# The first two pairs of the input projection k tile by k tile, the norms' squares and their weights moved, and y_b first in the attention

## The chip, the cores and the metric

One NeuronCore of one Trainium2 chip runs the whole kernel. The metric is the device time of one execution in microseconds (us). The five engines of the core work side by side, each through its own queue in order: TensorE (PE, with its weight loads shown apart as PEld), VectorE (DVE), ScalarE (ACT), GpSimd (POOL) and SyncE (SP), which here only issues DMAs.

## The reference, cut to what matters

One layer of a streaming encoder over 1024 tokens of width 1024, in float32:

```
h = rms_norm(x, norm_mix_pre)
q, k, v, u, gates = split(h @ w_in)            # 512 + 512 + 512 + 512 + 2048 columns
y_a = chunk_band_attention(q, k, v) @ w_attn_out   # 8 heads of 64, relative bias
y_b = multiscale_pool(u) @ w_pool_out
g_a, g_b = sigmoid(gates + b_gate)
x = x + rms_norm((g_a * y_a + g_b * y_b) @ w_o)
x = x + rms_norm(conv_gated_ffn(rms_norm(x)))
```

## The kernel before, in words

Every product is made of float32 numbers split in two (a high part rounded to the matmul's type, and the rest): `split` casts on ACT (line 78) and subtracts on DVE or POOL (line 79), and `mm3` (line 85) issues three matmuls of 128 x 128 by 512 columns for each k tile: high weight by high token, high by low, low by high. A block of 128 output columns over 512 tokens and all 8 k tiles is 24 matmuls.

The input projection runs over 16 pairs of output blocks (`IN_PAIRS`); each pair's weights are one load of 1 MB. Pairs 2 to 15 use a seven-product scheme of 2 x 2 blocks (class `Pair`, methods p1 to p7) on normalised, pre-added tokens (B11, T1, T2 and so on), which DVE and ACT make. Pairs 0 and 1 don't wait for the norms: they multiply the raw tokens (only scaled by the norm weights, `split_raw`, line 382), and the result is scaled per token afterwards (`evict_first`, line 437). The index i is the half of the k tiles (0 or 1, four tiles each), the index t or j the half of the tokens.

The order at the start (lines 358 to 371) is written out by hand: SP loads the tokens of (i, j) = (0, 0) in two pieces, all small columns (`cv`, 110 KB, with the norm weights in them), the weights of pairs 0 and 1 in pieces, the other token quarters, and then the eight row tiles `xn` for the norms. Lines 559 to 584 then do the products half by half: all of pair 0 for the first token half and i = 0 (bank X), pair 1 (bank Y), then i = 1, then the second token half (banks Z and Y). ACT takes the squares of all rows (`squares`, line 411), DVE makes the reciprocal roots (`scales`), `spread` lays them along the partitions through four PE transposes (line 424) and a DVE copy (line 426), and `normalise` (line 431) scales the raw tokens in place for the later pairs. The framework's list scheduler sets the order on each engine from the order of the program, from priorities (`tc.high_priority`) and from its own estimate of readiness.

PSUM has eight banks; a pool of tiles takes them in the order in which its tags are first named. In the projection that is X (banks 0, 1), Y (2, 3), Z (4, 5), m (6, 7). The attention's pools follow in the order psT (transposes, 2 banks), psf (y_b and the values, 2 banks), psS (scores, 2 x 2 banks), so that scores lie over Z and m. SBUF is used again in the same way: the attention's pool `atn` starts where the projection's operands T1, B11, B21, T2, ... lay, 16 KB for each high and low pair.

At the projection's end the last pair (products p1, p2, p6, p3, p7, p4 in this order) makes q and k of heads 6 and 7; `store_split` (lines 455 to 463) writes high and low parts with two DMAs each, for the last pair from POOL's queue. The attention goes through 32 steps (8 heads, 4 groups J of 256 queries) with the stages scores (lines 733, 742, softmax on DVE, ACT and POOL in 749 to 754), transposes (line 775) one step later, and values (line 800) two steps later. The pool branch's product y_b, cut in 32 units of 6 matmuls (tile ybp), is laid between them by a list `NU` written by hand, which says how many units each step takes. `load_head` loads q and k of a head (lines 705 to 709), `load_yb` a block of w_pool_out and the gates.

Of the kernel before, what the change touches and what calls it, by code (L numbers as in the profile page):

```python
# [10 lines left out]
F32 = mybir.dt.float32  # L11
F32R = mybir.dt.float32r
# [5 lines left out]
P = 128  # L18
# [3 lines left out]
DH = 64  # L22
# [11 lines left out]
C_GAIN = 212  # L34
NCOL = 220
# [12 lines left out]
def trunk(ctx, tc, xn, xt, w_in, cols, bias, w_ao, w_pg, w_po, w_o, gains, w_up, w_dn, out):  # L48
# [239 lines left out]
    def rstd_of(r, ssq, tmp, n, off=eps):  # L288
# [5 lines left out]
        A.activation(s, ssq, AF.Sqrt, scale=1.0 / D, bias=off)  # L294
# [7 lines left out]
        V.tensor_tensor(r, r, a, ALU.mult)  # L302

# [15 lines left out]
    with ExitStack() as ph:  # L319
# [33 lines left out]
        wr = [raw_tile(f"win{pi}") for pi in range(2)]  # L353
        wv = [w.rearrange("p (f q k c) -> p f q (k c)", f=2, q=2, k=4) for w in wr]
        wd = [w_in[pi].rearrange("p (f q n) -> p f q n", f=2, q=2) for pi in range(2)]
        q = {(i, j): raw_tile(f"xq{i}{j}").rearrange("p (k n) -> p k n", k=4)
             for j in range(2) for i in range(2)}
        nc.sync.dma_start(q[0, 0][:, 0:2], xt[0, 0][:, 0:2])
        nc.sync.dma_start(cv, cols)
        nc.sync.dma_start(wv[0][:, 0, 0], wd[0][:, 0, 0])  # L360
        nc.sync.dma_start(q[0, 0][:, 2:4], xt[0, 0][:, 2:4])
        nc.sync.dma_start(wv[0][:, 1, 0], wd[0][:, 1, 0])
        nc.sync.dma_start(wv[1][:, :, 0], wd[1][:, :, 0])
        nc.sync.dma_start(q[1, 0], xt[1, 0])
        for pi in range(2):
            nc.sync.dma_start(wv[pi][:, :, 1], wd[pi][:, :, 1])
# [9 lines left out]
        def gain(i, k):  # L376
            return cv[:, C_GAIN + 4 * i + k:C_GAIN + 4 * i + k + 1]

        def split_raw(i, j):
            hi, lo = XR[i, j]  # L380
            for k in range(4):
                A.activation(hi[:, k], q[i, j][:, k], AF.Identity, scale=gain(i, k))
                V.scalar_tensor_tensor(lo[:, k], q[i, j][:, k], gain(i, k), hi[:, k].bitcast(F32),
                                       ALU.mult, ALU.subtract)
# [3 lines left out]
        def split_in(pi, i):  # L388
            w = wr[pi].rearrange("p (f q k c) -> p f q k c", f=2, q=2, k=4)
            place = (lambda: tmp.tile([P, 2, 4, P], F32R, tag="o", name="w0s", bufs=4)) if pi == 0 else None  # L390
            for f in range(2):
                ws[pi, f, i] = split_w(w[:, f, i], f"i{pi}_{i}{f}", None, place)

        def half_in(pi, t, i, tag, fs=range(2)):


            for f in fs:
                if i == 0:
                    acc[pi, t, f] = psp.tile([P, 512], F32, tag=tag, name=f"i{pi}_{f}{t}")
                wh, wl = ws[pi, f, i]  # L400
                th, tl = XR[i, t]
                mm3(acc[pi, t, f], [wh[:, k] for k in range(4)], [wl[:, k] for k in range(4)],
                    [th[:, k] for k in range(4)], [tl[:, k] for k in range(4)], i == 0, i == 1)
# [5 lines left out]
        def squares(j):  # L409
# [3 lines left out]
        def scales(j):  # L413
            s = slice(4 * j, 4 * j + 4)
            rstd_of(rst[:, s], ssq[:, s], tmp, 4)

        def spread(j):

            s = slice(4 * j, 4 * j + 4)
            bc = tmp.tile([P, 4, P], F32, tag="S", name=f"bc{j}", bufs=4)  # L420
            V.tensor_copy(bc, rst[:, s].unsqueeze(2).to_broadcast([P, 4, P]))
# [4 lines left out]
            V.tensor_copy(Rb[j], ps)  # L426
# [38 lines left out]
        def evict_in(fb):  # L465
            def evict(f, t, ps, add):
# [10 lines left out]
                elif b < 16:  # L477
                    A.copy(d, ps)
# [821 lines left out]
```

## Time and profile before

| | |
|---|---|
| median of 3 runs | 1275.87 us (1274.69 to 1276.26) |
| the profiled execution | 1275.48 us |
| its span in the trace | 1273.7 us |
| TensorE (PE) busy | 1245.4 us, 98% |
| VectorE (DVE) busy | 907.6 us, 71% |
| ScalarE (ACT) busy | 667.3 us, 52% |
| GpSimd (POOL) busy | 313.9 us, 25% |

The profile is of one execution; its times start at the span's start. The share of an engine is an average over stages with different limits, so the views by stage and the list of waits say more than this table. The ends of matmuls are modelled: the distance between two starts is the sure quantity, not the length of one.

### The profile page before, as it was taken

Reading aid. Unit: us, or ns where it says so; the run is one execution under the profiler, and the core shown is the slowest. Engines: PE = TensorE matmul, PEld = TensorE weight load, DVE = VectorE, ACT = ScalarE, POOL = GpSimd, SP = SyncE. Lnnn points to the kernel's source line nnn. Section 1 sums busy time; section 2 is a strip of 40 time slices with the busy share of each in tenths; the row PEclk is TensorE's granted clock in tenths of the full one; section 3 lists DMA queues with packets and bytes.
Section 4 is the critical chain, followed back from the end, with each engine's and each line's share of the span. In section 5 each row is a group of like instructions: output and inputs, shape, how many; then the busy total and the mean of one; then the engine's idle time right before and its main releaser. Section 6 shows DMA issues by size and latency. Waiting matters only on the chain.

```text
span 1273.7 us, 16331 instructions
## 1 busy us (share of the span) xinstructions
PE 1245.4 (98%) x5780; PEld 1030.3 (81%) x5780; DVE 907.6 (71%) x1455; ACT 667.3 (52%) x1163; POOL 313.9 (25%) x270
## 2 busy tenths in 40 slices
PE   7999999999899999999999999999999999999997
PEld 6768887878788898888887888888888887888886
DVE  5894335875477777854799666666666676899958
ACT  7653245554477774433456555455455554445553
POOL 0005222322256556000034333333333310000000
PEclk9999999999999999999999999999999999999999
DMA  9345015344878965612142221221221259202103
GB/s 361 122 161 186 34 58 201 118 145 151 258 224 253 273 190 216 238 67 84 66 165 100 99 95 55 99 99 51 99 96 45 99 176 370 107 17 100 34 1 132
DMA packets 55857, 173.40 MB, mean 136 GB/s; under 512 B 5472, under 2 KB 6112, under 8 KB 50784
## 3 DMA queue, kind: packets, MB, share of 16 engines
q1 hardware_dynamic: 49424, 157.68, 35.8%
q10 hardware_dynamic: 4608, 8.39, 1.7%
q0 software_dynamic: 1744, 6.29, 1.3%
q8 instruction: 45, 0.74, 0.2%
q14 instruction: 36, 0.29, 0.1%
HBM read 125.16 MB, written 47.19 MB: 135 GB/s over the span
## 4 chain that ended last, share of the span: by engine, by line
PE 87%; DVE 6%; issue 3%; ACT 2%; DMA 1%; POOL 0%; DVEq 0%; ACTq 0%; SPq 0%; POOLq 0%
PE X_u L85 16%; PE X_i L85 9%; PE X L85 9%; PE Y_u L85 8%; PE wops L986 7%; PE Y L85 6%; PE Y_i L85 5%; PE Z_u L85 4%; PE y L85 4%; PE ybp L85 3%; PE i L85 3%; PE u L85 3%; PE f L800 2%; PE Z_i L85 2%; PE tp L775 2%
## 5 line engine op out<-in xcount | busy, mean ns | idle before, releaser
L1062 DVE SCALAR_TENSOR_TENSOR hc<-hu,cv,hc 128x1022 f32<-128x1022 f32 (+1 forms) x88 | 116.0, 1322 | 35.3 <-ACT hc L1057 35.2
L78 ACT CAST wh_u<-s_u 128x512 fp32r<-128x512 f32 x80 | 49.4, 618 | 78.7 <-PE Y_u L85 38.1
L79 DVE TENSOR_TENSOR wl_u<-s_u,wh_u 128x512 fp32r<-128x512 f32 x80 | 57.0, 714 | 39.8 <-ACT wh_u L78 39.7
L195 POOL TENSOR_TENSOR s_u<-wup 128x512 f32<-128x512 f32 x20 | 36.4, 1822 | 172.8 <-DMA wup<-in_w_up 127.1
L78 ACT CAST wh_u<-wup 128x512 fp32r<-128x512 f32 x72 | 44.6, 622 | 61.2 <-PE Y_u L85 29.0
L79 DVE TENSOR_TENSOR wl_i<-s_i,wh_i 128x512 fp32r<-128x512 f32 x56 | 41.4, 742 | 43.7 <-ACT wh_i L78 43.6
L78 ACT CAST wh_i<-s_i 128x512 fp32r<-128x512 f32 x56 | 34.7, 622 | 68.3 <-PE X_i L85 28.0
L199 POOL TENSOR_TENSOR s_u<-s_u,wup 128x512 f32<-128x512 f32 x20 | 28.1, 1407 | 137.6 <-DVE wl_u L79 137.5
L1057 ACT ACTIVATE hc<-hu,cv 128x1024 f32<-128x1024 f32 x44 | 54.6, 1243 | 10.9 <-DVE hu L1047 8.5
L195 POOL TENSOR_TENSOR s_i<-win 128x512 f32<-128x512 f32 x12 | 18.0, 1497 | 146.5 <-DVE wl_i L79 101.6
L79 DVE TENSOR_TENSOR wl_u<-wup,wh_u 128x512 fp32r<-128x512 f32 x72 | 50.4, 700 | 4.8 <-PE tp L311 2.0
L79 DVE TENSOR_TENSOR ptl<-tp,pth 128x512 fp32r<-128x512 f32 (+3 forms) x80 | 43.7, 555 | 13.7 <-ACT pth L78 12.5
L201 POOL TENSOR_TENSOR s_u<-wup 128x512 f32<-128x512 f32 x20 | 45.5, 2274 | 30.5 <-DVE wl_u L79 30.5
L754 POOL TENSOR_SCALAR pe<-pe,st 128x640 f32<-128x640 f32 (+2 forms) x64 | 43.0, 675 | 33.2 <-DVE st L753 28.3
L751 ACT ACTIVATE pe<-sm,st 128x640 f32<-128x640 f32 (+2 forms) x64 | 44.6, 698 | 6.3 <-DVE st L749 5.4
L78 ACT CAST wh_i<-win 128x512 fp32r<-128x512 f32 x42 | 25.7, 621 | 41.2 <-PE X_i L85 21.8
L1067 ACT ACTIVATE hc<-hc 128x1024 f32<-128x1024 f32 x22 | 23.4, 1064 | 40.6 <-DVE hc L1062 40.6
L749 DVE CUSTOM_DVE_ANT_0 sm<-pst,bt 128x640 f32<-128x640 f32 (+2 forms) x64 | 40.6, 651 | 4.2 <-PE pst L733 1.5
L85 PE MATMUL ybp<-mx,wh_yb 128*128 128x512 f32 x128 | 43.3, 418 | 0.0
L78 ACT CAST pth<-tp 128x512 fp32r<-128x512 f32 (+3 forms) x80 | 37.0, 472 | 9.4 <-PE tp L775 7.0
L775 PE MATMUL tp<-ident,pe 128*128 128x128 f32 x240 | 37.2, 278 | 0.4
L800 PE MATMUL f<-ptl,vv 128*128 128x256 f32 x144 | 36.8, 287 | 0.0
(521 smaller groups left out, 4193.9 us busy)
## 6 DMA issues: line engine op xcount, KB each, us to landing
wup<-in_w_up SPq DMA_DIRECT2D x22, 1024.0 KB, 4.9
win<-in_w_in SPq DMA_DIRECT2D x14, 1024.0 KB, 5.3
g_d<-hc SPq DMA_DIRECT2D x20, 512.0 KB, 2.6
sig_d<-d ACTq DMA_DIRECT2D x32, 256.0 KB, 2.0
a<-g_d SPq DMA_DIRECT2D x8, 1024.0 KB, 6.3
b<-in_w_dn SPq DMA_DIRECT2D x8, 1024.0 KB, 8.1
x<-in_xn SPq DMA_DIRECT2D x8, 512.0 KB, 12.8
v_d<-vt SPq DMA_DIRECT2D x8, 512.0 KB, 3.0
```

What stands on the lines that cost most here:

```text
L78: A.copy(hi, src)
L79: (eng or V).tensor_tensor(lo, src, hi.bitcast(F32), ALU.subtract)
L85: nc.tensor.matmul(ps, a[i], b[i], start=start and i == 0 and p == 0, stop=stop and i == n - 1 and p == 2, skip_group_check=True,)
L195: self.eng.tensor_tensor(self.s1, self.w21, self.w22, ALU.add)
L201: self.eng.tensor_tensor(self.s3, self.w11, self.w21, ALU.subtract)
L751: A.activation(pe[:, :n], sm[:, :n], AF.Exp, scale=-1.0, bias=st[:, 0:1], accum_out=st[:, 1:2])
L754: G.tensor_scalar(pe[:, :n], pe[:, :n], st[:, 2:3], 1.0, ALU.mult, ALU.mult)
L775: nc.tensor.transpose(tp[:, c * P:(c + 1) * P], pe[:, b * P:(b + 1) * P], ident)
L800: nc.tensor.matmul(fo, vv[:, kb, e].rearrange("p a d -> p (a d)"), t[:, s], start=s == slots[0] and x == 0, stop=s == slots[-1] and x == 1)
L986: nc.tensor.matmul(ps[:, 512 * c:512 * c + 512], a[k // 4][:, k % 4, sl], wo[k][b][:, 512 * c:512 * c + 512], start=k == 0 and x == 0, sto ...
L1057: A.activation(c, hu, AF.Identity, scale=cv[:, C_CW + 88 + b:C_CW + 89 + b], bias=cv[:, C_CB + b:C_CB + b + 1])
L1062: V.scalar_tensor_tensor(c[:, n:], hu[:, :S - n], cv[:, w:w + 1], c[:, n:], ALU.mult, ALU.add)
```

## The change

The diff below is cut to its core. In words:

- The weights of pairs 0 and 1 come in a layout of their own (`w_first`: for each k tile the 4 blocks of 128 columns side by side), and are loaded with the tokens k tile by k tile: pieces of 256 KB for the first two k tiles, 512 KB for the others. The norm weights become a load of 4 KB of their own (`gain_pre`) on ACT's queue; `cv` without them goes to the end of the opening loads, behind four of the row tiles, the second token half and the other four row tiles.
- For the first token half all four blocks (banks X, X, Y, Y) are done k tile by k tile, with the three products of a tile in the order high-high for the 4 blocks, high-low for the 4, low-high for the 4. ACT's instructions keep the order of the program here (`manual_schedule`): splits of the 8 k tiles, squares and root of the first four row tiles, raw split of the second half's i = 0, copy of the spread scales (now on ACT), raw split of i = 1, squares and root of the other four. The sigmoids of the first evictions come behind that second root.
- For the second half, blocks 0 and 1 (bank Z) go first, k tile by k tile, then blocks 2 and 3 one after the other (bank Y).
- `normalise` of the second half moves behind p2 of pair 2, and `evict_first(0, 1)` ahead of it.
- The tags of PSUM are named in the order m, Y, X, Z, and the attention's pools in the order psS, psT, psf: scores lie over m and Y, transposes over X, y_b and values over Z.
- `store_split` writes both parts with one DMA of SP, for the last pair too. One ACT instruction with Exp behind an eviction of pair 12 loads the exponential's table there.
- In the attention `load_yb(0)`, `load_head(0)`, the split of the first y_b weights and the scores of step 0 get high priority. The y_b weights move from pool `wrp` into `atn`, whose first tile they become. `NU` becomes 2, 2, 0, 1, 0, 1, 1, 2, then as before; the units of steps 0 and 1 are held behind the last score matmul of the step named in the diff.

```diff
 ...
+        for tag in "mYXZ":
+            psp.tile([P, 512], F32, tag=tag, name=f"bank{tag}")
+        gn = const.tile([P, 8], F32, name="gn")
+        A.dma_start(gn, gain_pre)
+        for c in (slice(0, 1), slice(1, 2), slice(2, 4)):
+            nc.sync.dma_start(q[0, 0][:, c], xt[0, 0][:, c])
+            nc.sync.dma_start(wr[0][:, c], w_first[0][:, c])
+        for c in (slice(0, 2), slice(2, 4)):
+            nc.sync.dma_start(q[1, 0][:, c], xt[1, 0][:, c])
+            nc.sync.dma_start(wr[1][:, c], w_first[1][:, c])
+        for n in range(4):
+            nc.sync.dma_start(xts[n], xn[n])
         for i in range(2):
             nc.sync.dma_start(q[i, 1], xt[i, 1])
-        for n in range(8):
+        for n in range(4, 8):
             nc.sync.dma_start(xts[n], xn[n])
+        nc.sync.dma_start(cv, cols)
 ...
+        def products(bs, t, i, k):
+            wh, wl = ws[i, k]
+            th, tl = XR[i, t]
+            for p, (w, x) in enumerate(((wh, th), (wh, tl), (wl, th))):
+                for b in bs:
+                    nc.tensor.matmul(acc[b, t], w[:, b], x[:, k], start=i == k == p == 0,
+                                     stop=i == 1 and k == 3 and p == 2, skip_group_check=True)
 ...
             Rb[j] = out_tile(f"R{j}")
-            V.tensor_copy(Rb[j], ps)
+            A.copy(Rb[j], ps)
 ...
+                kk = [(i, k) for i in range(2) for k in range(4)]
+                for b, tag in enumerate("XXYY"):
+                    bank(b, 0, tag)
+                with tc.manual_schedule(engines={nc.scalar.engine}):
+                    for i, k in kk:
+                        split_raw(i, 0, k)
+                        split_first(i, k)
+                        if (i, k) != kk[-1]:
+                            products(range(4), 0, i, k)
+                    load_win(2)
+                    load_win(3)
+                    scales(0)
+                    for k in range(4):
+                        split_raw(0, 1, k)
+                    spread(0)
+                    products(range(4), 0, 1, 3)
+                    for k in range(4):
+                        split_raw(1, 1, k)
+                    root = scales(1)
+                for b in range(2):
+                    bank(b, 1, "Z")
+                with tc.issue_after(root.ins):
+                    evict_first(1, 0)
+                    evict_first(0, 0)
                 for i in range(2):
                     normalise(i, 0)
+                for n, (i, k) in enumerate(kk):
+                    products(range(2), 1, i, k)
+                    if n == 4:
+                        spread(1)
+                for b in (2, 3):
+                    bank(b, 1, "Y")
+                for b in (2, 3):
+                    for i, k in kk:
+                        products((b,), 1, i, k)
 ...
                 pair.p1()
                 operand("B21", q[1, 0])
+                evict_first(0, 1)
                 pair.p2()
+                for i in range(2):
+                    normalise(i, 1)
                 nxt.p1()
 ...
-            eng.dma_start(hd, hi.bitcast(F32))
-            eng.dma_start(ld, lo.bitcast(F32))
+            nc.sync.dma_start(dst.rearrange("a p n -> p a n"), d.bitcast(F32))
 ...
+                if (f, t, fb) == (1, 1, IN_PAIRS[-4]):
+                    A.activation(warm, d[:, :1], AF.Exp, scale=0.0)
 ...
         atn = pool(ph, "attn", 2)
+        psS = pool(ph, "psS", 2, space=PSUM)
         psT = pool(ph, "psT", 2, space=PSUM)
         psf = pool(ph, "psf", 1, space=PSUM)
-        psS = pool(ph, "psS", 2, space=PSUM)
 ...
-            wr = load_block(w_po, m, "yb")
-            sg = sgs[m] if m in sgs else atn.tile([P, S], F32, tag="sg", name=f"sgb{m}")
+            wr = atn.tile([P, 4, P], F32, tag="wy", name=f"wr_yb{m}")
+            nc.sync.dma_start(wr, w_po[m])
+            sg = atn.tile([P, S], F32, tag="sg", name=f"sgb{m}")
 ...
-        load_head(0)
-        load_yb(0)
+        with tc.high_priority():
+            load_yb(0)
+            load_head(0)
+            first_yb = split_w(ybs[0][1], "yb0", V)
+            pend = {0: scores(0, 0)}
 ...
-        NU = [0, 1, 1, 2] * 7 + [0, 1, 1, 1, 1, 0]
+        NU = [2, 2, 0, 1, 0, 1, 1, 2] + [0, 1, 1, 2] * 5 + [0, 1, 1, 1, 1, 1]
 ...
+            if i == 1:
+                with tc.issue_after(last["pst"].ins):
+                    for _ in range(NU[i]):
+                        next(units)
             if 1 <= i <= len(steps):
                 transposed(steps[i - 1][1], pend.pop(i - 1))
-            for _ in range(NU[i]):
-                next(units, None)
+            if i == 0:
+                with tc.issue_after(last["pst"].ins):
+                    for _ in range(NU[i]):
+                        next(units)
+            elif i > 1:
+                for _ in range(NU[i]):
+                    next(units, None)
 ...
```

## Rows read from the trace of the kernel before

**Rows 1.** The page: busy time, share and instructions of each engine; the granted clock in 40 slices of the span.

```profile
PE 1245.4 (98%) x5780; PEld 1030.3 (81%) x5780; DVE 907.6 (71%) x1455; ACT 667.3 (52%) x1163; POOL 313.9 (25%) x270
PEclk9999999999999999999999999999999999999999
```

**Rows 2.** The waits of PE over the whole span: who waited for whom, us in total, times, longest us.

```profile
PE i L85 <- ACT w0s L78: 7.5, 1, 7.5
PE pst L742 <- DVE d L476: 3.1, 1, 3.1
```

**Rows 3.** Busy time by stretch: the stretch in us, its length, then busy us and instructions of PE, PEld, DVE, ACT, POOL, and last the granted clock, the DMA engines' share and GB/s.

```profile
7.40:13.30 5.90, 5.81 (x14) 4.33 (x15) 4.28 (x7) 3.02 (x6) 0.00 (x0) 1.00 1.02 387
30.00:36.00 6.00, 6.00 (x30) 4.94 (x29) 0.15 (x1) 4.29 (x7) 0.00 (x0) 1.00 0.81 331
45.00:97.00 52.00, 48.45 (x207) 37.45 (x206) 51.95 (x66) 29.72 (x43) 1.67 (x1) 1.00 0.33 117
341.10:344.40 3.30, 0.23 (x2) 0.04 (x1) 1.29 (x2) 0.63 (x2) 0.81 (x2) 1.00 1.00 349
344.40:351.40 7.00, 6.15 (x21) 5.24 (x22) 4.03 (x17) 4.86 (x12) 4.00 (x14) 0.51 1.00 301
361.50:480.00 118.50, 118.14 (x782) 105.12 (x781) 93.58 (x262) 89.58 (x217) 68.52 (x93) 1.00 0.80 230
```

**Rows 4.** The chain of waits in its first microseconds: start us, length us, what.

```profile
1.18 4.33 DMA cv<-in_cols
...
6.93 0.52 ACT w0s L78
...
7.49 27.89 PE i L85 x108
```

**Rows 5.** The timeline of PE at the start; each row is the second of three matmuls of a k tile, so two rows are three matmuls apart.

```profile
9.44 0.63 PE L85 MATMUL i<-XR00l,w0s 128*128 128x512 f32 x1
10.72 0.63 PE L85 MATMUL i<-XR00l,w0s 128*128 128x512 f32 x1
...
14.03 0.39 PE L85 MATMUL i<-XR00l,w0s 128*128 128x512 f32 x1
14.73 0.40 PE L85 MATMUL i<-XR00l,w0s 128*128 128x512 f32 x1
```

**Rows 6.** The DMA view of the first 80 us: GB/s in 40 slices of 2 us; issues with KB each and the median us from issue to landing.

```profile
GB/s 18 265 228 335 380 416 401 434 422 406 404 414 408 410 424 412 426 156 223 205 231 262 135 0 0 0 0 41 221 8 0 0 0 187 206 131 0 0 131 0
...
sig_d<-d ACTq DMA_DIRECT2D x10, 256.0 KB, 2.1
...
cv<-in_cols SPq DMA_DIRECT2D x1, 110.0 KB, 4.3
```

**Rows 7.** The instructions that read the raw tokens, the first weights and the row tiles, in the first 50 us: ns min/median/max, first and last start.

```profile
L382 ACT ACTIVATE XR00h<-xq,cv x4: 705/714/722, 5.6 to 9.0; 128x512 fp32r<-128x512 f32 x4
L78 ACT CAST w0s<-win x4: 601/602/615, 6.8 to 16.4; 128x512 fp32r<-128x512 f32 x4
...
L411 ACT ACTIVATE sq<-x x8: 1042/1060/1062, 23.0 to 31.9; 128x1024 f32<-128x1024 f32 x8
```

**Rows 8.** The timeline of DVE: start us, us, line, operation, idle before it and its releaser.

```profile
29.53 0.43 DVE L421 COPY bc<-rst 128x512 f32<-128x512 f32 x1
35.85 0.69 DVE L426 COPY R<-rps 128x512 f32<-128x512 f32 x1 [5.90 <-PE rps L424]
```

**Rows 9.** The timeline of PE: the transposes of the first spread and the first matmul of pair 2.

```profile
35.22 0.60 PE L424 MATMUL rps<-ident,bc 128*128 128x128 f32 x4
...
55.46 0.39 PE L85 MATMUL X_i<-B11h,wh_i 128*128 128x512 f32 x1
```

**Rows 10.** The chain of waits in the projection's middle: 12 matmuls at the full pace.

```profile
102.35 2.72 PE Y_i L85 x12
```

**Rows 11.** The timeline of PE around the projection's end: the last matmul of p2, the last of p4, and the first scores.

```profile
330.03 0.39 PE L85 MATMUL Z_i<-B21h,wl_i 128*128 128x512 f32 x1
...
340.91 0.39 PE L85 MATMUL Z_i<-T4h,wl_i 128*128 128x512 f32 x1
344.36 0.72 PE L742 MATMUL pst<-kh,qs 128*128 128x256 f32 x2 [3.07 <-DVE d L476]
```

**Rows 12.** The timelines of ACT (first and last row) and DVE in the same place.

```profile
342.37 0.62 ACT L78 CAST hi<-d 128x512 fp32r<-128x512 f32 x1 [3.16 <-DMA q_d<-hi]
...
343.02 0.69 DVE L79 TENSOR_TENSOR lo<-d,hi 128x512 fp32r<-128x512 f32 x1 [3.09 <-ACT hi L78]
343.63 0.68 DVE L476 TENSOR_TENSOR d<-Z_i,p_i 128x512 f32<-128x512 f32 x1
...
345.02 1.28 ACT L751 ACT_TABLE_LOAD   x1
```

**Rows 13.** SP's DMA issues there (first and last load of head 0's q and k, and the first load behind them), and from the DMA view of 300 to 360 us the median time to landing of such loads.

```profile
327.79 0.50 SPq L705 DMA_DIRECT2D qs<-q_d  x1
...
330.90 0.59 SPq L707 DMA_DIRECT2D kl<-k_d  x1
...
341.33 0.34 SPq L657 DMA_DIRECT2D wr_yb<-in_w_po  x1
...
kl<-k_d SPq DMA_DIRECT2D x4, 256.0 KB, 7.3
...
vv<-v_d POOLq DMA_DIRECT2D x1, 1024.0 KB, 9.2
```

More of the change, by code (lines that the diff above doesn't have):

```diff
@@ L47, in trunk @@
 @with_exitstack
-def trunk(ctx, tc, xn, xt, w_in, cols, bias, w_ao, w_pg, w_po, w_o, gains, w_up, w_dn, out):
+def trunk(ctx, tc, xn, xt, w_first, w_in, cols, gain_pre, bias, w_ao, w_pg, w_po, w_o, gains, w_up, w_dn, out):
     nc = tc.nc
@@ L293, in rstd_of @@
         V.tensor_scalar(v, ssq, 1.0 / D, off, ALU.mult, ALU.add)
-        A.activation(s, ssq, AF.Sqrt, scale=1.0 / D, bias=off)
+        root = A.activation(s, ssq, AF.Sqrt, scale=1.0 / D, bias=off)
         V.reciprocal(r, s)
@@ L302, in rstd_of @@
         V.tensor_tensor(r, r, a, ALU.mult)
+        return root
     def transpose_to(q, src, t, ps_tile, ev="AA"):
@@ L376, in gain, with split_raw, split_first, bank @@
         def gain(i, k):
-            return cv[:, C_GAIN + 4 * i + k:C_GAIN + 4 * i + k + 1]
-        def split_raw(i, j):
+            return gn[:, 4 * i + k:4 * i + k + 1]
+        def split_raw(i, j, k):
             hi, lo = XR[i, j]
[L381 to L384, printed above, removed]
+            A.activation(hi[:, k], q[i, j][:, k], AF.Identity, scale=gain(i, k))
+            V.scalar_tensor_tensor(lo[:, k], q[i, j][:, k], gain(i, k), hi[:, k].bitcast(F32),
+                                   ALU.mult, ALU.subtract)
         ws, acc = {}, {}
[L388 to L403, printed above, removed]
+        def split_first(i, k):
+            place = (lambda: tmp.tile([P, 2, 4, P], F32R, tag="o", name="w0s", bufs=4)) if i == 0 else None
+            ws[i, k] = split_w(wr[i][:, k].rearrange("p (b c) -> p b c", b=4), f"first{i}{k}", None, place)
+        def bank(b, t, tag):
+            acc[b, t] = psp.tile([P, 512], F32, tag=tag, name=f"i_{b}{t}")
+        def products(bs, t, i, k):
[5 more added lines that the diff above has]
+                                     stop=i == 1 and k == 3 and p == 2, skip_group_check=True)
         ssq = tmp.tile([P, 8], F32, tag="ssq", name="ssq", bufs=1)
@@ L573, in trunk @@
-                with tc.high_priority():
-                    for j in range(2):
-                        squares(j)
-                        scales(j)
-                half_in(0, 1, 0, "Z", (0,))
-                spread(0)
-                for n in range(2):
-                    evict_first(n, 0)
-                half_in(0, 1, 0, "Z", (1,))
-                half_in(0, 1, 1, "Z", (0,))
+                kk = [(i, k) for i in range(2) for k in range(4)]
+                for b, tag in enumerate("XXYY"):
+                    bank(b, 0, tag)
@@ L697, in load_head @@
             qs = atn.tile([P, S], F32R, tag="qs", name=f"qs{h}")
-            if h == 0:
-                sgs[0] = atn.tile([P, S], F32, tag="sg", name="sgb0")
             kh = atn.tile([P, S], F32R, tag="kh", name=f"kh{h}")
@@ L732, in scores @@
                         for x, kk in enumerate((kh, kl)):
-                            nc.tensor.matmul(
+                            last["pst"] = nc.tensor.matmul(
                                 pst[:, 512 * c:512 * c + 320], qs[:, j * P:(j + 1) * P],
@@ L741, in scores @@
                     for x, kk in enumerate((kh, kl)):
-                        nc.tensor.matmul(pst[:, :nn], qs[:, j * P:(j + 1) * P], kk[:, :nn],
+                        last["pst"] = nc.tensor.matmul(pst[:, :nn], qs[:, j * P:(j + 1) * P], kk[:, :nn],
                                          start=x == 0, stop=x == 1)
@@ L785, in transposed @@
                     split(hi, lo, tp[:, c * P:(c + n) * P].rearrange("p (b q) -> p b q", b=n))
-        avs = {}
+        avs, last = {}, {}
         def values_of(h, J):
```

72 lines of the change are left out of this document (19 added, 53 removed).

## The prediction

> **What bounds the kernel now.** I read the page first: PE is busy 98% of the span and no other engine passes 71%, so a change can gain only where PE stands still or runs slowly, some 28 us in all [rows 1]. PE's waits say where: 7.5 us for the first weights, 3.1 us at the first scores, the rest in pieces of about a microsecond [rows 2]. Next I cut the span into stretches [rows 3].
>
> At the start the chain goes through the load of cv, which lands at 5.5 us, then casts of tokens and of the first weights on ACT, and PE begins at 7.49 [rows 4]. From there three matmuls take 1.28 us, 0.43 each, which is the 1.2 GHz level, and from 13.3 on 0.70, or 0.23 each, which is 2.4 GHz [rows 5]. The granted clock reads 1.00 in that stretch all the same [rows 3], so here the spacing tells the level, not that column.
>
> From 45 to 97 us DVE is busy 51.95 of 52.0 us while PE is busy 48.45 [rows 3]: DVE bounds this stretch and costs PE 3.55 us. Yet shortly before, from 30 to 36 us, DVE did almost nothing [rows 3]: the broadcast scales were ready at 29.96, their PE transposes stood at 35.22 behind other matmuls, and DVE waited 5.90 us [rows 8, 9].
>
> At the change to the attention PE ends its last product at about 341.1 and starts the first scores at 344.36 [rows 11]. The reason is a chain in DVE's queue: the store of a q block was slow, ACT waited 3.16 us for its buffer, DVE's subtraction waited for ACT, and the eviction of bank Z, over which the scores lie, came behind it [rows 12]. After that pause the granted clock is 0.51 for 7.0 us (the 1.2 GHz level for nearly all of it) and PE idles another 0.85 us [rows 3]. So 3.3 of pause, 0.85 of idle, and 6.15 busy us of which about 0.49 would go away at the full clock (3.0): 7.2 us lost. Afterwards PE is busy 118.14 of 118.50 us [rows 3], so time gained here isn't waited for again.
>
> **The start.** Before its first matmul PE now needs 256 KB of tokens, 256 KB of weights and the 4 KB of norm weights; cv is out of the way. The first two slices of 2 us moved 18 and 265 GB/s, together 0.57 MB by 4.0 us [rows 6]; the two pieces are 0.52 MB, so tokens at about 3.0 and weights at 3.9. One cast of tokens 0.71, one of weights 0.60 [rows 7]: first matmul at about 4.6 to 5.0; I take 4.9, a gain of 2.6. The unknown is the small load on ACT's queue. From the ACT start near 0.7 it lands at 3.0 if it goes like the quick stores (2.1), at 5.4 if like cv (4.33) [rows 4, 6]. It is most like the stores, since nothing of ACT's queue is ahead of it and it is the smaller one; the other end makes the start 6.9 and the gain 0.6. The best end, weights at 3.3, gives 2.9. The load is ahead of the sqrt table on ACT, 0.3 us that end before the tokens land.
>
> Afterwards PE can't starve: a k tile is 12 matmuls, 5.1 us at the low level or 2.7 at the high one [rows 5, 10], against 1.3 us for its 0.52 MB at 400 GB/s [rows 6] and 1.3 us on ACT [rows 7]. I leave the slow stretch at 5.8 us; from 13.3 the spacing changes at once, so a shorter one by 2 us would give 1 us, a longer one take 1.
>
> Here a rule speaks against the change. The Trainium skill, DMA: Bandwidth & Descriptors, section Bandwidth, wants transfers of at least 1 MiB, and has 341 GB/s for 1 MB against 138 for 64 KB. By 138 GB/s the first two pieces would take an estimated 3.8 us instead of some 2, and the start would gain under 1 us. The trace's opening, with pieces of 110 to 512 KB, moved 228 to 335 GB/s per slice after the first [rows 6], which is nearer to the large figure.
>
> **The DVE stretch.** ACT's fixed order puts four squares and the root ahead of the second raw split. The first four row tiles end 6.3 MB of loads, near 19 us by the slices of some 400 GB/s [rows 6]; with the last square of 1.06 [rows 7], the root and five small DVE steps the scales are ready at about 22 us (an estimate). Spread's transposes stand in the program ahead of the last 12 matmuls of the first token half. PE reaches them after 84 matmuls: 4.9 + 5.8 slow (13.6 of them) + 70 x 0.227 = 26.6 us; before, they came at 35.2 [rows 9]. ACT copies the scales (the DVE copy of 0.69 goes, twice). DVE's work that needs the scales starts at 28 to 30 instead of 35.85 [rows 8], 6 to 8 us earlier, and is 1.4 us shorter. To free PE it must be ahead by the earlier start of PE, 2.6, plus the whole waiting, 3.55: 6.15. It just is. But the order on DVE changes too, and the first split of pair 2 gets its buffer only some 9 matmuls (2 us) before PE needs it, since all four weight buffers serve until the last block. Both ends: 1.0 (order spoils it) and 3.55; I take 2.9, near the upper end, because the slack of 5.9 us [rows 8] exceeds the need.
>
> What could be late next is ACT: its copy of the scales waits for PE's transposes until 27.2, and behind it in the fixed order stand the raw split of i = 1 (four casts, 2.9 us) and four squares. PE wants that split only after 12 + 24 matmuls, at about 35; it is there from 29 to 31. The second spread needs the root at about 35.5, PE comes to it at about 36.5; if it is 1 us late, PE loses up to 1, which the range holds. The sigmoids behind that root delay only stores. SP: cv is wanted at 36, lands behind 10 MB, near 27; the next weights were free anyway.
>
> **The change to the attention.** Scores now lie over m and Y. Y's last product p3 ends two products (5.4 us [rows 10]) ahead of p4, which is Z's, and m was free long before; so the first scores need only their loads, and PE fills with 4 units of y_b, 24 matmuls, 5.4 us [rows 10], whose bank and operands are free earlier. That covers the first softmax chain, and with no pause the clock has no reason to fall. The exponential's table (1.28 us [rows 12]) moves into ACT idle time in pair 12; without that cover it would push a weight split by 1.3, two products ahead of its use. One store DMA of SP in place of two of POOL: POOL is freed, SP issues four more, and nobody waits for heads 6 and 7 for 100 us. The high-priority loads (nine DMAs) pass SP's stores; a store held behind a load keeps one of four buffers, no more. load_head(1) no longer stands behind wr_yb, which waited on SP until 341.33 [rows 13].
>
> Upper end 7.2. Lower end 3.5: the pause goes but 0.85 stays and steps 2 to 4, which lose 2 units of cover (2.7 us [rows 10]), wait for the softmax. I take 6.3, near the upper end: the attention's steps ran with 0.36 us of idle in 118 [rows 3].
>
> **The sum.** 2.6 + 2.9 + 6.3 = 11.8. Against the profiled execution's own 1275.5 (span 1273.7 and 1.8 around it): 1263.7. The median of the runs is 0.4 above that execution, so 1264.1.
>
> **Rivals.** (a) The opening gains little: the small load or the small pieces land late (0.6) and DVE's order keeps PE waiting (1.0). For it: the slow cv row [rows 4]. Against: the DMA slices [rows 6]. Then 1275.9 - 0.6 - 1.0 - 6.3 = 1268.0. The rule of the Trainium skill on large transfers (DMA: Bandwidth & Descriptors, section Bandwidth) is of this kind.
>
> (b) The change doesn't do what it says in the attention: the scheduler lays y_b or the scores where they still wait, and only the 3.5 us or less comes. For it: in this stretch loads take 7.3 us and up to 9.2 [rows 13]. Against: the loads are placed first. Then 1275.9 - 5.5 - 3.5 = 1266.9, or 1270.4 with nothing at all.
>
> (c) Slower: the high-priority scores stand in PE's queue right behind p2 and wait there for head 0, with p6, p3, p7 and p4 behind them. Place: kl now lies over B21, so it can't be issued before p2 ends at 330.3 [rows 11]; four more DMAs of 0.6 and 9.2 to land [rows 13] make 341.9, a wait of 11.6; and after a pause the next 7 us run at the low level, 3.5 lost [rows 3]: 15.1 in place of the 7.2. It decides when it exceeds 7.2, the opening's gain and 2.6 for a visible loss. With the opening at its lower end (1.6) that is from 11.4 on, and gives 1275.9 - 1.6 + 7.9 = 1282. Against it: before, with its own loads issued at 327.8 to 331.5 [rows 13], the scheduler kept scores behind everything. With a good opening it ends near 1278.
>
> **Chances.** Forecast 0.72, its own range 1261 to 1267; (a) 0.10; (b) 0.10; (c) 0.05; gains and waits that cancel, 0.03. What a measurement of this kernel can tell from no change is 0.2%, 2.6 us. Faster by more 0.90, within 0.05 (the cancelling and part of (b) and (c)), slower 0.05. Range 1261 to 1270.5: the low end is all upper ends (2.9 + 3.55 + 7.2 = 13.7) and a slow stretch shorter by 2 us, the high end is (b) with nothing from the attention.
>
> **What would show it.** Right: first matmul between 4.6 and 5.2, spacing 0.23 from about 10.7; the rps transposes near 27 and the first X_i near 52.9; PE idle from there to 97 under 1 us; no pause of PE near 335, ybp rows between the first pst rows, and a granted clock of 1.00 there. Wrong: a first matmul near 7; PE waiting on DVE for more than 2 us up to 100; a PE wait for qs, kh or kl ahead of the last Z_i; a granted clock near 0.5 at the first scores; or, in steps 2 to 4, PE waits for pe.

## The result and the profile after

The change makes the kernel slower: 1282.02 us median of 5 runs (1279.62 to 1282.64) against 1275.72 of the kernel before in the same runs, ratio 1.0049, 95% interval 1.0035 to 1.0064. The profiled execution after took 1282.64 us, span 1280.5, so 6.8 us more span than before (1273.7). Forecast was 1264.1. Single executions at a lower clock or far longer than the rest (the profiled one of e5, 1388.33 us at a mean clock of 0.848, one of e13 and a few of the kernel before) are left out of all ratios below.

The page, as [rows 1]: PE does as much work as before; in slice 11 of 40 (320 to 352 us) its busy share falls to 5 tenths and its granted clock to 8. Rows: busy time by engine; PE's busy tenths by slice; its granted clock by slice.

```profile
PE 1244.4 (97%) x5780; PEld 1029.0 (80%) x5780; DVE 909.0 (71%) x1453; ACT 666.0 (52%) x1164; POOL 309.4 (24%) x262
...
PE   8999999999599999999999999999999999999997
...
PEclk9999999999899999999999999999999999999999
```

PE's waits over the whole span, as [rows 2] (who waited for whom, us in total, times, longest us):

```profile
PE pst L747 <- DMA kh<-k_d: 12.7, 1, 12.7
PE i L405 <- ACT w0s L77: 6.1, 1, 6.1
...
PE m_i L84 <- ACT wh_i L77: 1.2, 1, 1.2
...
PE m_i L84 <- DVE wl_i L78: 1.0, 1, 1.0
```

One wait outweighs all else: the first scores wait 12.7 us for kh of head 0, where [rows 2] had 3.1 for an eviction. PE's timeline there, as [rows 11]:

```profile
336.74 0.39 PE L84 MATMUL Z_i<-T4h,wl_i 128*128 128x512 f32 x1
349.80 0.77 PE L747 MATMUL pst<-kh,qs 128*128 128x256 f32 x2 [12.67 <-DMA kh<-k_d]
```

Why kh is late stands in SP's own timeline (its DMA issues, x2 joins two), as [rows 13]:

```profile
328.47 6.15 SPq L463 DMA_DIRECT2D q_d<-hl  x2
337.22 0.36 SPq L463 DMA_DIRECT2D k_d<-hl  x1
337.67 0.42 SPq L721 DMA_DIRECT2D wr_yb<-in_w_po  x1
...
339.02 0.52 SPq L709 DMA_DIRECT2D qs<-q_d  x1
339.64 0.54 SPq L710 DMA_DIRECT2D kh<-k_d  x1
...
342.14 0.59 SPq L711 DMA_DIRECT2D kl<-k_d  x1
```

Three of the last input pair's stores stand ahead of head 0's loads. Each store waits for an eviction, the third for that of p7, which is ready at 337.20. Until then SP issues none of head 0's loads; the first qs goes out at 339.02, where [rows 13] has 327.79, and PE was through at 336.97. Then the transfers take their time: by the chain of waits the last kl, issued at 342.14, takes 8.57 us to land, just ahead of the second pair of score matmuls at 350.84.

The stretches, as [rows 3] (stretch, its length, busy us of PE, PEld, DVE, ACT, POOL, granted clock, DMA share, GB/s):

```profile
45.00:97.00 52.00, 48.96 (x209) 38.45 (x208) 49.91 (x60) 31.32 (x45) 3.54 (x3) 1.00 0.44 155
...
349.80:356.80 7.00, 6.72 (x18) 5.31 (x19) 1.28 (x9) 0.99 (x4) 0.85 (x2) 0.52 1.06 267
361.50:480.00 118.50, 116.86 (x784) 103.79 (x782) 92.59 (x265) 90.08 (x220) 69.98 (x95) 1.00 0.79 235
```

After the pause the granted clock is 0.52 for 7 us, the 1.2 GHz level, just as it was 0.51 after the shorter pause before. The account, from the last matmul of p4 to the first matmul of wops behind the attention: 202.0 us after (336.74 to 538.7) against 191.0 before (340.91 to 531.9), 11.0 more. Of these about 9.6 are the longer pause (12.8 against 3.2), 0.2 the slow stretch and 1.3 idle time from 361.5 to 480 (1.64 against 0.36). Up to the last matmul of p4 it is 4.2 us ahead (336.74 against 340.91); 11.0 - 4.2 = 6.8.

### The profile page after: what moved, and what is told of

Read it like the earlier page. It is cut to its first block, busy times and chain, and to the rows that moved or that the text cites. A ratio compares the mean times of both kernels' runs of the same rounds, so it can differ in the third digit from the quotient of the medians.

```text
span 1280.5 us, 16292 instructions
## 1 busy us (share of the span) xinstructions
PE 1244.4 (97%) x5780; PEld 1029.0 (80%) x5780; DVE 909.0 (71%) x1453; ACT 666.0 (52%) x1164; POOL 309.4 (24%) x262
## 4 chain that ended last, share of the span: by engine, by line
PE 88%; DVE 5%; ACT 2%; issue 2%; DMA 2%; POOL 1%; SPq 0%; DVEq 0%; ACTq 0%; POOLq 0%
PE X_u L84 16%; PE X_i L84 10%; PE X L84 9%; PE Y_u L84 8%; PE wops L1002 7%; PE Y L84 6%; PE Y_i L84 5%; PE Z_u L84 4%; PE i L405 4%; PE y L84 3%; PE u L84 3%; PE ybp L84 3%; PE Z_i L84 2%; PE f L805 2%; PE tp L780 2%
## 5 line engine op out<-in xcount | busy, mean ns | idle before, releaser
L1073 ACT ACTIVATE hc<-hu,cv 128x1024 f32<-128x1024 f32 x44 | 54.6, 1244 | 10.6 <-DVE hu L1063 8.1
L805 PE MATMUL f<-pth,vv 128*128 128x256 f32 x144 | 36.2, 285 | 0.0
```

The costliest lines, as they stand in the source:

```text
L805: nc.tensor.matmul(fo, vv[:, kb, e].rearrange("p a d -> p (a d)"), t[:, s], start=s == slots[0] and x == 0, stop=s == slots[-1] and x == 1)
L1073: A.activation(c, hu, AF.Identity, scale=cv[:, C_CW + 88 + b:C_CW + 89 + b], bias=cv[:, C_CB + b:C_CB + b + 1])
```

## The experiments

Twelve kernels, each timed beside the kernel before; its median was 1274.93 with e1 to e4, 1275.18 with e5 to e9, 1274.94 with e10 to e12, 1275.24 with e13. Ratios are to it. The changed kernel was timed beside 1275.72, so a difference to its 1282.02 is some 0.5 to 0.8 us too large. Medians and means of one kernel differ by up to 0.7 us, and the intervals reach some 1 us to either side, so a difference of 1 us between two kernels tells little.

| kernel | median us | ratio, 95% interval |
|---|---|---|
| e1 stores on GpSimd | 1273.06 | 0.9987 [0.9977, 0.9996] |
| e2 opening alone | 1273.19 | 0.9987 [0.9978, 0.9997] |
| e3 e1, old y_b list | 1273.59 | 0.9988 [0.9978, 0.9997] |
| e4 attention alone, stores on GpSimd | 1275.29 | 1.0004 [0.9995, 1.0013] |
| e5 stores on ScalarE | 1276.20 | 1.0006 [0.9998, 1.0015] |
| e7 e5, old y_b list | 1277.53 | 1.0019 [1.0011, 1.0028] |
| e8 before, stores on ScalarE | 1279.99 | 1.0037 [1.0024, 1.0049] |
| e9 e5, first loads spread otherwise | 1276.75 | 1.0012 [1.0004, 1.0021] |
| e10 loads ahead of the stores | 1269.70 | 0.9966 [0.9954, 0.9979] |
| e11 e10, old y_b list | 1272.71 | 0.9983 [0.9974, 0.9992] |
| e12 e10, old opening | 1272.63 | 0.9984 [0.9975, 0.9992] |
| e13 e10, y_b's casts early | 1269.84 | 0.9962 [0.9948, 0.9975] |

**e1.** The changed kernel with the last pair's stores back on GpSimd's queue.

```diff
-            nc.sync.dma_start(dst.rearrange("a p n -> p a n"), d.bitcast(F32))
+            eng.dma_start(dst.rearrange("a p n -> p a n"), d.bitcast(F32))
...
+                eng = G if fb == IN_PAIRS[-1] else nc.sync
```

> The changed kernel with one edit: the last pair's four stores of q and k go out from POOL's queue again (still one DMA for both parts), so none of them stands in SP's queue ahead of head 0's loads. Theory A (SP's queue order: the loads were issued at 337.7 instead of 327.8 us because they stand behind three stores that wait for the last evictions): first load issued by 325, scores at most 1 us behind the last projection product (near 337), granted clock 1.00 there, and the 12.95 us wait with the 3.2 us of slow clock behind it gone: 1282.0 - 16.1 = 1266, 1264 to 1268. Rival B (kl's new place over B21, issued only behind p2, and loads of 7 to 9 us): the loads go out at 326 to 329, land near 338 to 342, PE still waits 1 to 5 us and the clock falls again: 1269 to 1276. Rival C (the loads are late through traffic on the DMA engines, whoever issues what): no change, 1280 or more.

Measured 1273.06, 9.0 us under the change. Head 0's loads went out from 323.59 to 328.74, and the first scores came at 336.90, straight behind p4. But a new wait appears at the first transposes. GpSimd's timeline:

```profile
328.19 0.90 POOL L698 DMA_DIRECT2D vv<-v_d  x1 [21.20 <-DVE wl_i L78]
...
343.00 0.73 POOL L463 DMA_DIRECT2D k_d<-hl  x1 [7.81 <-DVE st L759]
...
346.54 2.05 POOL L760 TENSOR_SCALAR pe<-pe,st 128x128 f32<-128x128 f32 x4
```

and PE's:

```profile
346.97 0.48 PE L781 MATMUL tp<-ident,pe 128*128 128x128 f32 x1 [3.77 <-POOL pe L760]
```

A store whose data were ready at 337.13 went out at 343.00, the next, ready at 339.16, at 345.48, and the scaling of the exponentials, which PE's tp needs, stands behind both. Why they went out so late is not settled: the rows name DVE, but vv, the 1 MB load ahead of them in that queue, took 14.5 us and landed at 342.7, 0.3 before the first of the two.

**e2.** The kernel before with the new opening and nothing of the attention's part (gn, w_first, the k tiles of the first pairs, the squares and scales; stores, tiles, PSUM order and y_b list as before).

```diff
-                split_raw(0, 0)
-                split_in(0, 0)
-                half_in(0, 0, 0, "X")
...
+                    for i, k in kk:
+                        split_raw(i, 0, k)
+                        split_first(i, k)
+                        if (i, k) != kk[-1]:
+                            products(range(4), 0, i, k)
```

> The kernel before with the change's opening alone (loads, products k tile by k tile, order of squares, splits and normalise); attention, stores and PSUM order as before. Theory A (the opening kept its gain and the loss is all behind the projection's end): PE ends the projection 4.2 us earlier, as in the changed kernel, and the total is 1275.7 - 4.2 = 1271.5, 1270.5 to 1272.5. Rival D (the opening's gain is given back later): 1274 to 1276.

Measured 1273.19, between the two expectations: the opening is worth 1.7 us, not the 5.5 of the forecast. In the profiled execution the last matmul of p4 is 3.5 us ahead of the kernel before (337.42 against 340.91) and the first of wops 2.7 (529.2 against 531.9), so part of the gain is given back behind the projection, where this kernel still has a wait of 3.0 at its scores.

**e3.** e1 with the list of y_b units per step as before.

```diff
-        NU = [2, 2, 0, 1, 0, 1, 1, 2] + [0, 1, 1, 2] * 5 + [0, 1, 1, 1, 1, 1]
+        NU = [0, 1, 1, 2] * 7 + [0, 1, 1, 1, 1, 0]
```

> The kernel of e1 with the list of y_b units per step as before (0, 1, 1, 2 repeated), so no y_b ahead of the first transposes. If y_b first is what covers the first softmax chain, PE stands 2 to 4 us between the first scores and the first transposes and the clock may fall: 2 to 6 us slower than e1. If the first scores' early place is enough: within 1 us of e1.

Measured 1273.59, within noise of e1: PE waits 4.3 for GpSimd's pe and 2.9 for a softmax in place of e1's 3.8. While the queue is blocked, filling in front of it is worth little.

**e4.** e1 with the opening of the kernel before, so e2's diff taken back:

```diff
-                        split_first(i, k)
...
+                split_in(0, 0)
+                half_in(0, 0, 0, "X")
```

> The kernel before with the change's attention alone (PSUM order, early loads and scores, y_b first, one store DMA) and the last pair's stores on POOL as in e1; the opening as before. If the parts add up: e1's time plus the opening's 4.2, near 1270 by theory A. If the attention needs the other opening: 1273 or more.

Measured 1275.29: with the stores on GpSimd the attention's part is worth nothing (longest tp wait for pe 4.9). e1 and e4 differ by 2.2, the opening.

**e5.** e1 with these stores on ScalarE's queue.

```diff
-                eng = G if fb == IN_PAIRS[-1] else nc.sync
+                eng = A if fb == IN_PAIRS[-1] else nc.sync
```

> The changed kernel with the last input pair's four stores on ScalarE's own DMA queue, neither on SP (the change) nor on GpSimd (the kernel before and e1). Theory: what the attention lost in the changed kernel and again in e1 is one queue each time: on SP the stores hold head 0's loads, on GpSimd the store of k_d (idle 7.8 us at 343.0 in e1's trace) holds the copies of the exponentials behind it, so TensorE's first tp waits 3.77 us and runs at the slow level until 350. On ScalarE's queue nothing is behind a store but work that comes after it anyhow. Expected: first pst directly behind the last Z_i at about 336.9, no wait of tp over 1.5 us, last Z_i to the start of the tail's wops about 188 us (e1 191.8, before 191.0), time about 1269 (ratio to before 0.995). Rival: the loads of head 0 are late for want of bandwidth (11 to 12 us to land in e1), and pst or tp waits as long again, for them or for bias: time as e1's, 1273.

My theory failed: 1276.20, 3.1 slower than e1. The trace is read from e9, whose attention is the same. SP's waits from 318 to 352 us there:

```profile
SPq L712 <- DMA q_d<-hl: 6.5, 1, 6.5
...
SPq L711 <- DMA k_d<-hl: 4.0, 2, 3.1
```

Loads on SP wait for stores on ScalarE to land, though they read other blocks. That is shown; what couples the two queues is argued. By the program's instruction list, which no trace holds, the DMAs of SP and ScalarE take eight completion counts in turn, in program order over both queues, and each waits for the DMA that had its count last; GpSimd's DMAs have counts of their own. e1's trace agrees: SP's later loads wait for the one eight places ahead of them in that queue (y_b's next weights, L722, for the first bias load; the gate behind them, L724, for the qs behind that bias load), and none waits for a store on GpSimd. SP's waits there from 318 to 352 us:

```profile
SPq L722 <- DMA bt<-in_bias: 2.5, 1, 2.5
SPq L724 <- DMA qs<-q_d: 1.5, 1, 1.5
```

So a load can stand behind a store even from another queue. The rival, want of bandwidth, fell too: the loads weren't issued.

**e7.** e5 with the old y_b list (e3's two lines).

> As e5_stores_act, with the old list of y_b units per step (none of y_b's matmuls between the first scores and their transposes). If y_b first is what fills the wait for the first softmax, TensorE has nothing between the second pst and the first tp: a wait of 3 to 5 us there and slow matmuls behind it, 3 to 4 us more than e5, about 1272. Rival, that y_b first is worth nothing as e3 against e1 seemed to show (0.5 us, while GpSimd's queue was blocked in both): the same time as e5 within 1 us.

Measured 1277.53, 1.3 slower than e5, nearer to the rival. PE waits 8.6 us for kh in this trace and in e9's, so there is little for y_b to fill.

**e8.** The kernel before with e5's two lines and nothing else.

> The kernel before, with only the last input pair's stores moved from GpSimd's queue to ScalarE's. The prediction took the 3.1 us pause of TensorE at 341 (and the 0.85 us and the slow matmuls behind it, 7.2 us in all) for a thing of the order of TensorE's work. Theory now: part of it is GpSimd's blocked queue, as in e1. If so the first scores come 2 to 3 us earlier and the time is 1271 to 1273. Rival: the pause stays where it is, and the time is the kernel before's, 1275.

Measured 1279.99, 4.8 slower than before, again a miss. SP's waits from 318 to 352, and PE's timeline at the first scores:

```profile
SPq L707 <- DMA q_d<-hi: 9.5, 1, 9.5
```

```profile
346.93 0.77 PE L742 MATMUL pst<-kh,qs 128*128 128x256 f32 x2 [6.92 <-DMA kh<-k_d]
```

The same hold, in a kernel that has nothing of the change. It shows what putting these stores on GpSimd did for the kernel before; where its own pause of 3.1 us comes from it does not show.

**e9.** e5 with the first loads issued otherwise: norm weights first on SP, the first weights piece on ScalarE's queue.

```diff
-        A.dma_start(gn, gain_pre)
+        nc.sync.dma_start(gn, gain_pre)
...
-            nc.sync.dma_start(wr[0][:, c], w_first[0][:, c])
+            (A if c.start == 0 else nc.sync).dma_start(wr[0][:, c], w_first[0][:, c])
```

> As e5_stores_act, with the opening's first loads spread over two queues in another way: the norm weights first on SP, the first piece of the weights first on ScalarE's queue, so that it is issued at about 0.75 in place of 1.18 us. The prediction put the first matmul at 4.9 and it came at 6.10, behind the cast of a piece that landed at 5.43. Theory: the landing of that piece is what sets it. Expected: it lands about 0.4 us earlier, first matmul at about 5.6, time as e5's less 0.4 or less. Rival: x's piece (now issued behind the norm weights) becomes the later one, and the first matmul stays at 6.1 or later.

The rival was right. Weights landed 3.1 us after issue and norm weights 1.7, but the token piece, issued at 1.17, came only at 6.14, and the first matmul at 7.42; 1276.75, as e5. ScalarE's timeline:

```profile
6.14 0.72 ACT L384 ACTIVATE XR00h<-xq,gn 128x512 fp32r<-128x512 f32 x1 [3.91 <-DMA xq<-in_xt]
```

**e10.** The changed kernel with one order on SP's queue turned round, by four ordering edges: the last pair's stores behind head 0's bias load.

```diff
...
-            nc.sync.dma_start(bt, bias[h])
+            bl = nc.sync.dma_start(bt, bias[h])
+            if h == 0:
+                for st in stores[-4:]:
+                    after_load(st, bl)
```

> The changed kernel with one order turned round and nothing else: on SP's queue head 0's loads (y_b's weights and gate, q, k, bias) stand ahead of the last input pair's four stores, in place of behind three of them. The stores stay on SP, GpSimd and ScalarE issue none. Theory: the 12.7 us wait of the first scores in the changed kernel is this order alone. Expected: loads issued from 323 to 329 as in e1, first pst directly behind the last Z_i at about 337, and no tp held by a GpSimd store as in e1 (3.8 us there); last Z_i to wops about 188 us, time about 1269 (ratio to before 0.995). Rival: q, k and bias are late for want of bandwidth whatever the order (11 to 12 us to land in e1), so that a wait of 3 to 4 us stays at the first tp: time as e1's, 1273.

Measured 1269.70, ratio 0.9966 [0.9954, 0.9979]: 12.3 us under the change by the medians, and 10.6 when the mean of each is set against the kernel before in its own runs (6.3 above, 4.3 below). That comes from an order alone, and it is faster than the kernel before. SP's timeline:

```profile
325.63 0.51 SPq L714 DMA_DIRECT2D qs<-q_d  x1
...
329.44 0.53 SPq L718 DMA_DIRECT2D bt<-in_bias  x1
330.35 4.90 SPq L464 DMA_DIRECT2D q_d<-hl  x2
337.84 2.40 SPq L464 DMA_DIRECT2D k_d<-hl  x2
```

and PE's:

```profile
337.36 0.39 PE L84 MATMUL Z_i<-T4h,wl_i 128*128 128x512 f32 x1
337.59 0.40 PE L755 MATMUL pst<-kh,qs 128*128 128x256 f32 x2
...
339.70 0.73 PE L84 MATMUL ybp<-mx,wh_yb 128*128 128x512 f32 x2 [1.28 <-ACT wh_yb L77]
...
343.14 1.05 PE L84 MATMUL ybp<-mx,wh_yb 128*128 128x512 f32 x2
343.99 0.63 PE L84 MATMUL ybp<-mx,wl_yb 128*128 128x512 f32 x1
```

No pause is left but 1.28 us for y_b's cast; behind it two y_b matmuls take 0.85 us, 0.43 each, the 1.2 GHz level. No store waits harmfully: the loads are out by 330, before the second store's data exist. From p4's end to wops it is 191.1 us all the same (337.36 to 528.5), not the 188 expected.

**e11.** e10 with the old y_b list (e3's two lines).

> As e10_loads_first, with the old list of y_b units per step: 6 of y_b's matmuls between the first scores and the first tp in place of 24. Tells what y_b first is worth when no queue is blocked. If it fills the wait for the first softmax: 3 us or more slower than e10 with a wait of tp of that size. Rival: no difference over 1 us, as between e7 and e5 (1.3 us) and e3 and e1 (0.5 us).

Measured 1272.71: 3.0 us slower than e10 by the medians, 2.2 by the means. That is nearer to the first theory, though the wait is at the second scores, not at tp. PE's waits from 337 to 530:

```profile
PE pst L755 <- DVE st L762: 2.6, 2, 2.4
```

So y_b first is worth 2 to 3 us; e3 and e7 show 0.5 and 1.3, behind blocked queues. The profiled executions don't show it, since e10's was the slowest of its five: wops starts at 528.2 here and at 528.5 in e10.

**e12.** e10 with the opening of the kernel before (e4's lines).

> As e10_loads_first, with the opening of the kernel before: the attention part alone, in its unblocked form. The prediction put 6.3 us on the attention and 5.5 on the opening. With e2 (the opening alone gained 1.7 us): time e10 plus 1.7 to 2.2, so about 1271, and 4 us under before for the attention. Rival: the attention part is worth nothing here too (e4: 0.4 us slower than before), 1275.

Measured 1272.63, between theory and rival: the attention's part is worth 2.3 us in its unblocked form, the opening 2.9 on top of it (2.2 both by the means). PE's waits from 337 to 545, against [rows 2] and the 0.85 us idle behind the pause:

```profile
PE pst L752 <- DMA kl<-k_d: 1.0, 1, 1.0
PE tp L785 <- POOL pe L764: 0.8, 2, 0.6
PE pst L752 <- DVE st L759: 0.6, 1, 0.6
PE ybp L85 <- POOL wl_yb L79: 0.5, 1, 0.5
PE tp L785 <- DVE ptl L79: 0.4, 1, 0.4
PE ybp L85 <- ACT wh_yb L78: 0.3, 1, 0.3
PE tp L785 <- DVE st L763: 0.2, 1, 0.2
```

The stretch from the end of p4 to wops (columns as [rows 3]), of the kernel before and of e12:

```profile
341.10:531.90 190.80, 186.52 (x1106) 161.53 (x1105) 145.48 (x341) 123.49 (x280) 101.88 (x127) 0.98 0.75 234
```

```profile
339.40:528.50 189.10, 184.87 (x1106) 158.42 (x1105) 144.16 (x341) 121.44 (x278) 98.93 (x115) 1.00 0.77 239
```

PE is idle 4.28 us before and 4.23 in e12. The one pause was cut up, not removed; what is gained here, 1.65 us of busy time for the same 1106 instructions, is the clock, which stays at 1.00 through these eight small waits. As much again of e12's gain lies ahead of this stretch: its p4 ends 1.7 us earlier than before (last matmul 339.24 against 340.91) with the old opening, 1.25 of it between 97 us and there.

**e13.** e10 with y_b's first two casts ahead of the last evictions' work on ScalarE and VectorE, by the same kind of edges.

```diff
...
+            for i in range(2):
+                for x in late[-3:]:
+                    after_load(x[i], splits[-1][i])
+            for x in adds[-2:]:
+                after_load(x, splits[-1][1])
```

> As e10_loads_first, with the two casts of y_b's first weights (ScalarE and VectorE) ahead of the last evictions' work on those engines in place of behind it. In e10's trace the weights landed at 328.0, ScalarE is idle from 330.2 to 333.5 and VectorE from 329 to 332, yet the cast stands behind the last store's cast at 339.04, TensorE waits 1.28 us for it, and the 12 matmuls after it take 4.7 us in place of 2.7 at the full clock. Theory: this is the rest of what the attention's start loses. Expected: no wait of ybp, no stretch at the slow level behind the last Z_i, last Z_i to wops 188 to 189 us (e10 191.1), time about 1267.5 to 1268.5 (ratio to before 0.994 to 0.995). Rival: TensorE then reaches the first tp sooner and waits there for the softmax, whose bias lands at 339.9 in any case; half or more of it is given back and the time is e10's, 1269.7, or better by less than 1 us.

Measured 1269.84, no difference from e10. The profiled execution did what was expected, with the y_b rows at full pace (three matmuls in 0.77) and 188.4 us from the end of p4 to wops (336.11 to 524.5):

```profile
337.65 0.70 PE L87 MATMUL ybp<-mx,wh_yb 128*128 128x512 f32 x2 [0.68 <-ACT hl L79]
...
338.42 0.62 PE L87 MATMUL ybp<-mx,wh_yb 128*128 128x512 f32 x2
```

But the slow stretch that it removes was in e10's profiled execution (1272.57, mean clock 0.995) and, to judge by time and mean clock alone, hardly in e10's other four runs (1269.61 to 1270.52, clock 0.998). I had priced an execution, not the kernel. e10 and e13 are the fastest versions, 11 to 12 us under the change and 4 to 5 under the kernel before.

## Why the prediction was wrong

**The step that failed** is the sentence on SP's queue: "SP issues four more, and nobody waits for heads 6 and 7 for 100 us", and "the high-priority loads (nine DMAs) pass SP's stores". I asked who reads what the moved stores write. The question was who stands behind them on the queue that they are moved to. The loads did not pass the stores; they came behind three of them. They kept PE waiting 12.7 us at the scores, with 7 us at the low level behind it. e10, which turns just that order round, takes back 12.3 us (10.6 by the means); it is shown.

**Rival (c)** had the sign, the kind of wait (PE in order, waiting for head 0's loads, then 7 us at the low level) and the size: 15.1 forecast, 12.7 of wait and 3.2 of slow clock measured (6.72 us at 0.52). Its place was wrong: PE's scores stand behind p4, not p2, and it was SP's queue that was late, not the buffer under kl: e1 and e10 have these loads out by 330. That its 1282 is the measured time is luck: it took 1.6 us for the opening and 7.9 more loss behind it, where the traces have 4.2 ahead at p4's end and 11.0 lost after it. With chances of 0.05 it was far too cheap, and the row that should have raised it was on the table: before, the last pair's stores are on GpSimd and head 0's loads leave SP from 327.79 [rows 13], ahead of evictions that run past 343 [rows 12].

**The attention, 6.3.** Even unblocked it is 2.3 (e12), and of the 3.4 us by which e12's wops come earlier (528.5 against 531.9) only 1.7 arise in the attention. I took the steps to run with 0.36 us of idle in 118 [rows 3], as before; from 361.5 to 480 us e12 has 1.50, and over the attention idle time came to the same 4.2 us. Only the clock's part (3.0 at most) was real, 1.65 of it. The lower end, 3.5, was named for cover that y_b no longer gives to later steps; it was the nearer one, and still above what was measured. But lost cover is not shown as the reason: in that stretch e1, with the same list, is idle 0.45 us and e11, with the old list, 1.90. What makes the late waits stays open.

**The start, 2.6.** First matmul at 6.10, a gain of 1.4, then about the same slow stretch as before. The chain of waits, as [rows 4], and the DMA view of 0 to 80 us, as [rows 6] (first row) and of 0 to 12 us:

```profile
1.18 4.23 DMA wfirst<-in_w_first
...
5.43 0.63 ACT w0s L77
...
6.10 6.08 PE i L405 x14
```

```profile
GB/s 22 218 247 405 397 346 414 416 418 418 434 406 412 408 395 446 401 152 8 0 266 262 0 0 0 197 313 14 0 8 262 7 124 262 131 0 0 35 96 0
```

```profile
wfirst<-in_w_first SPq DMA_DIRECT2D x2, 256.0 KB, 4.9
gn<-in_gain_pre ACTq DMA_DIRECT2D x1, 4.0 KB, 3.7
```

The flow was somewhat below the forecast, 0.48 MB by 4.0 us in place of 0.57. The larger error was to give it all to the first two pieces, 0.52 MB: those behind them were in flight as well, and the piece of 256 KB, issued at 1.18, landed at 5.41, when by the slices 0.83 MB had moved. The Trainium skill (DMA: Bandwidth & Descriptors, section Bandwidth) wants pieces of 1 MiB and would have put the gain under 1 us; the measured 1.4 lies between that and mine, while the slices moved 218 to 247 GB/s, far above the 138 that it has for 64 KB. A slice holds several transfers, so that is no test of the figure; the piece alone, 256 KB in 4.23 us, came at 62 GB/s. The small load took 3.7 us on ScalarE's queue and 1.7 as the first on SP's (e9).

**The DVE stretch, 2.9.** The steps came as foretold: the transposes of the first spread at 28.14 (27 forecast, 35.22 in [rows 9]), DVE 2.0 us less busy. Yet PE's idle time from 45 to 97 fell only from 3.55 to 3.04. What is late next is not ACT's copy of the scales but a weight split: ScalarE's timeline at 68 us, then VectorE's.

```profile
68.11 0.59 ACT L224 COPY c<-m_i 128x512 f32<-128x512 f32 x1 [0.40 <-PE m_i L84]
...
68.59 0.62 ACT L77 CAST wh_i<-w 128x512 fp32r<-128x512 f32 x1
```

```profile
69.13 1.22 DVE L78 TENSOR_TENSOR B22l<-xq,B22h 128x1024 fp32r<-128x1024 f32 x1
70.27 0.68 DVE L78 TENSOR_TENSOR wl_i<-w,wh_i 128x512 fp32r<-128x512 f32 x1
```

The cast stands behind the copy of a finished product, the subtraction behind an operand of a later one, and PE waits 1.2 and 1.0 us for them: the order that the lower end of 1.0 had allowed for. The gain is 0.5 here. From 97 us to the end of p4 PE is idle 0.97 us against 2.40 before, which I had not counted; half of that is not the opening's, since e2 keeps 1.70. With the start the opening is worth 1.7 to 2.9 (e2, e1 against e4, e10 against e12), 5.5 forecast. Without the order on SP the sum would have been 11.8 forecast against 5.2 measured (e10; 4.3 by the means).

## What to carry to other kernels

When a store moves to another queue, ask what stands behind it there and when its data are ready; its reader may be 100 us away and the queue still be stopped. Loads that open a stage belong ahead of the stores that close the last one, and a scheduler's priority doesn't settle that: an explicit edge gave 11 to 12 us. A pause that is filled may come back as small waits elsewhere; its worth is then the clock that stays up.

## What the runs showed of the hardware

- The three queues gave three times for the same four stores: SP 1282.02, GpSimd 1273.06, ScalarE 1276.20 us. The Trainium skill (DMA: Bandwidth & Descriptors, section Issuing engines are not separate DMA queues) says that several issuing engines only save time of the sequencer. No run here tests that for the transfers alone; but which queue a store is issued on, and its place there, decided what waited for it, and that was worth up to 9 us, or 12.3 with the order on SP (e10).
- With SP's loads and GpSimd's transfers in flight together, landing took 11 to 15 us (medians in e1 from 310 to 350 us: kl 11.2, bias 12.4, vv 14.5) where [rows 13] has 7.3 and 9.2.
- Eight waits of 0.2 to 1.0 us left the granted clock at 1.00 (e12); one of 1.28 in e10's profiled execution was followed by matmuls at up to 0.43 us, the 1.2 GHz level, until 344.4. Its other runs, with a mean clock of 0.998 in place of 0.995, probably don't have that stretch; no trace shows them.
